# Keeping the scan inputs in SBUF, one array of token columns, positions added by TensorE, and the third part of the modulation moved to a later group

## The chip, the cores and the metric

The kernel runs on one core of a Trainium2 chip. The metric is the device time of one execution in microseconds (us), the median of several runs. In the profile PE is TensorE's matmuls, PEld its weight loads, DVE VectorE, ACT ScalarE, POOL GpSimd, and SP the engine from whose queue nearly every DMA of this kernel is issued.

## The reference: one layer of a hybrid model

2048 latent tokens and 128 context tokens, 1024 wide, pass through one layer. A position embedding is added to the latent tokens only: its first 512 columns depend on the token's grid row (64 tokens share one), the last 512 on its grid column.

```python
x_lat = x_sample + grid_pos_embed(x_sample.shape[1])
sh1, sc1, gt1, sh2, sc2, gt2 = split(silu(c) @ w_ada + b_ada, 6)     # for c and for c_ctx
h = rmsnorm(x, norm_mix) * (1 + sc1) + sh1
u, z_s5, qkv, z_gdn, beta_raw, a_raw = split(h @ w_in)
x = x + gt1 * (concat[s5(u, z_s5), deltanet(conv(qkv), z_gdn, ...)] @ w_out)
h = rmsnorm(x, norm_mlp) * (1 + sc2) + sh2
x = x + gt2 * (square(relu(h @ w_mlp_in)) @ w_mlp_out);  y = rmsnorm(x, norm_final)
```

`s5` is a complex diagonal state-space scan in both directions, `deltanet` a chunked gated delta rule, also in both directions. Everything is fp32; most products are made as three products of a high and a low part (`wh`, `wl` of a weight, `H`, `L` of the tokens).

## The kernel before

Tokens are cut into 17 tiles of 128; tile 16 is the context. The program runs in these stages; the order of instructions inside an engine is set by a scheduler that simulates the program as it is written, so code that moves also moves what is around it.

- **First phase** (`norm_rows`, `first_cols`, `first_pass`). `load_x` brings a tile of rows, adds the row part of the position on POOL (L205, from 64 equal copies of each row that a DMA with a zero step makes, L193) and the column part on DVE (L206). The rows are normalized (L182, L184, L80, L243), transposed on PE (L165), scaled and shifted on DVE (L172), split in high and low parts (L174 on ACT, L175 on POOL or DVE) and written to DRAM in four overlapping arrays per part, one for each later group, whose edge columns are written twice (L259, L263, L266). Eight blocks of tokens, `UBLOCKS` (the first has three tiles, the others two), are then multiplied on PE with the columns for `u` (L289), and ACT copies each result out of PSUM into a buffer `eu` (L292), of which there are two, that a DMA writes to the array `u` in DRAM (L294). The columns for the gates follow (L298 to L313, `gates`). Between the blocks the tables of the S5 scan are built (`s5_setup`, `s5_tables`: L1017 to L1249).
- **Modulation** (`modulation(k, b)`): `silu(c)` for both conditions times a third of `w_ada`, 2048 columns, loaded as 16 pieces of 512 KB (L131), each feeding two matmuls at different column positions of the array (L134). Third 0 runs before the first block, thirds 1 and 2 (`mods`) beside group 0.
- **Group 0** (`group_h`, `group_proj`): the token columns of five tiles are loaded from DRAM (L376), twelve blocks of 128 weight columns are split (L402 to L404) and saved (L387), multiplied (L471) and passed through the convolution (L491 to L503). Beside it run the first S5 scans (L1263 to L1364).
- **Groups 3, 1 and 2**: the same with weights loaded from what was saved, and beside it the inverses of the delta rule in three side sequences `first`, `second`, `third`, of which `third` (`gdn_second`, L775 to L813) uses the one PSUM bank `g3`.
- Then the remaining columns, the delta rule's steps, and the output projection and MLP of all tokens, which take more than half of the time.

All DMAs stand in one queue, SP's, in order: an instruction that waits there holds back all behind it.

Of the kernel before, what the change touches and what calls it, by code (L numbers as in the profile page):

```python
# [67 lines left out]
def setup_first(k):  # L68

    nc = k.nc  # L70
    cst = k.pa.tile([128, 528], F32, name="cst0")
    nc.sync.dma_start(cst, k.I['cst'][:, 512:1040])
    k.pos_c = cst[:, 0:512]
    k.eye16 = cst[:, 512:528]
# [35 lines left out]
def modulation(k, b):  # L110

    nc, I = k.nc, k.I
    bias = k.pm.tile([128, 512], F32, name="mbias")
    nc.vector.memset(bias, 0.0)
    ba = I['b_ada']
    for j in range(4):
        nc.sync.dma_start(bias[32 * j:32 * j + 2], dap(ba, (4 * b + j) * 512, [[0, 2], [1, 512]]))
    nrm = None
    if b != 1:
        nrm = k.pm.tile([128, 512], F32, name="mnorm")  # L120
        nc.vector.memset(nrm, 0.0)
        src = I['norm_mix'] if b == 0 else I['norm_mlp']
        for j in range(2):
            r0 = (64 if b == 0 else 0) + 32 * j
            nc.sync.dma_start(nrm[r0:r0 + 2], dap(src, j * 512, [[0, 2], [1, 512]]))
    ps = k.psM.tile([128, 512], F32, name="gA")
    for kk in range(8):
        for jp in range(2):
            w = k.pmw.tile([128, 2, 512], F32, name="wada")
            c0 = b * 2048 + jp * 1024  # L130
            nc.sync.dma_start(w.rearrange("p j c->p (j c)"), I['w_ada'][0][kk * 128:kk * 128 + 128, c0:c0 + 1024])  # L131
            for i in range(2):
                j = 2 * jp + i
                nc.tensor.matmul(ps[32 * j:32 * j + 32, :], k.csil[:, kk, :], w[:, i, :],  # L134
                                 start=(kk == 0), stop=(kk == 7), tile_position=(0, 32 * j))
            yield None
    rows = bias
# [5 lines left out]
    ps = k.psM.tile([128, 512], F32, name="gA")  # L143
# [52 lines left out]
def load_x(k, t):  # L196
# [13 lines left out]
UBLOCKS = ((16, 0, 1), (2, 3), (4, 5), (6, 7), (8, 9), (10, 11), (12, 13), (14, 15))  # L210


def place(t):

    if t == 16:
        return 0, 1
    return (0, 130 + 128 * t) if t < 4 else (t // 4, 1 + 128 * (t % 4))
# [29 lines left out]
def first_cols(k, tiles, early):  # L247

    nc, S = k.nc, k.S
    H = k.ph.tile([128, 8, 384], FR, name="uH")  # L250
    L = k.ph.tile([128, 8, 384], FR, name="uL")
# [3 lines left out]
    for part, X in (("hH", H), ("hL", L)):  # L255
        X = X.bitcast(F32)
# [13 lines left out]
def first_pass(k, early):  # L270

    nc, S = k.nc, k.S
    pend = []
    cols = first_cols(k, UBLOCKS[0], early)
    for bi, tiles in enumerate(UBLOCKS):
        n = 128 * len(tiles)
        H, L = cols
        if bi < 7:
            cols = first_cols(k, UBLOCKS[bi + 1], early)
        if bi < 6:  # L280
            early.update((t, norm_rows(k, t)) for t in UBLOCKS[bi + 2][:k.ahead])
        yield None
        for ct in range(4):
# [1588 lines left out]
```

## Time and profile before

| | us |
|---|---|
| median of 3 runs | 3313.88 |
| lowest, highest | 3308.87, 3318.6 |
| profiled execution | 3305.27 |
| its span from first to last instruction | 3303.5 |
| PE busy | 2998.2 |
| DVE busy | 2060.2 |

The profiled execution is one run of its own; sums over the trace are made against it and not against the median. "Busy" counts the time in which at least one instruction of an engine is in flight. A row of a group of instructions names line, engine, operation, what is written from what, shape and count, then the busy time and the mean of one, and the idle time of the engine just before them with what ended it.

### The profile page before, as it was taken

The numbers are of one execution on the slowest core, as the hardware profiler recorded it, in microseconds if no ns is written. First come the engines' busy times: TensorE is split into PE (matmuls) and PEld (weight loads), VectorE is DVE, ScalarE is ACT, GpSimd is POOL, SyncE is SP. The second block draws the span as 40 slices with busy tenths as digits, with TensorE's granted clock in tenths as the row PEclk, the third lists the DMA queues.
The fourth block names the chain that finished last, engine by engine and source line by source line (L and its number), as shares of the span: only waits on it lengthen the run. The fifth ranks groups of instructions, "written<-read, shape, count | busy, mean of one in ns | idle before, by whom it ended". The sixth has DMA issues, their size and how long they took to land.

```text
span 3303.5 us, 53799 instructions
## 1 busy us (share of the span) xinstructions
PE 2998.2 (91%) x19962; PEld 2637.7 (80%) x19962; DVE 2060.2 (62%) x4093; ACT 1115.0 (34%) x2517; POOL 1370.5 (41%) x1027
## 2 busy tenths in 40 slices
PE   5775879999798899988999999999999999999998
PEld 3673668787787777977997899898798898899997
DVE  4965587896876775346555368543368652685555
ACT  3432224443443221245323243322243332432332
POOL 3552232433345242155443453434444444554442
PEclk8887889998997999998999999999999999999999
DMA  9899966867677988999333545222435334453322
GB/s 258 197 179 250 335 205 228 266 217 236 201 217 233 285 286 273 345 307 312 107 103 112 156 147 178 81 76 92 143 99 184 112 102 127 155 166 93 99 90 71
DMA packets 573527, 604.69 MB, mean 183 GB/s; under 512 B 163020, under 2 KB 422208, under 8 KB 573264
## 3 DMA queue, kind: packets, MB, share of 16 engines
q1 hardware_dynamic: 573264, 601.25, 59.4%
q8 instruction: 157, 2.57, 0.3%
q14 instruction: 106, 0.87, 0.1%
HBM read 458.99 MB, written 142.14 MB: 182 GB/s over the span
## 4 chain that ended last, share of the span: by engine, by line
PE 56%; DVE 19%; DMA 14%; issue 4%; ACT 3%; POOL 3%; SPq 2%; POOLq 0%; DVEq 0%; ACTq 0%
PE gA L1523 20%; PE gA L1545 18%; PE d L471 6%; PE gA L1437 3%; PE gs L1356 1%; DVE W L738 1%; DVE Tt L1301 1%; DMA x<-in_posr 1%; DVE UB L736 1%; DMA woraw<-in_w_out 1%; DVE S L1338 1%; PE gs L1283 1%; POOL wol L1400 1%; DVE S L1303 1%; DMA s_stab<-WI 1%
## 5 line engine op out<-in xcount | busy, mean ns | idle before, releaser
L1400 POOL TENSOR_TENSOR wol<-woraw,woh 128x512 fp32r<-128x512 f32 x320 | 426.3, 1343 | 679.9 <-ACT woh L1399 669.5
L1530 DVE TENSOR_TENSOR r<-r 128x256 f32<-128x256 f32 (+1 forms) x256 | 290.7, 1168 | 363.8 <-ACT ffH L1529 363.6
L1399 ACT ACTIVATE woh<-woraw 128x512 fp32r<-128x512 f32 x320 | 194.4, 628 | 794.6 <-PE gA L1545 462.0
L1545 PE MATMUL gA<-woh,ffH 128*128 128x512 f32 x1088 | 426.8, 392 | 8.8 <-ACT r L1527 4.8
L1545 PE MATMUL gA<-woh,ffL 128*128 128x512 f32 x1088 | 425.3, 391 | 1.1 <-DVE ffL L1531 1.1
L1545 PE MATMUL gA<-wol,ffH 128*128 128x512 f32 x1088 | 424.2, 390 | 0.0
L1550 DVE TENSOR_TENSOR acc<-acc,gA 128x512 f32<-128x512 f32 x510 | 336.1, 681 | 123.7 <-PE gA L1545 123.6
L1400 POOL TENSOR_TENSOR wil<-wiraw,wih 128x1024 fp32r<-128x1024 f32 x128 | 318.9, 2491 | 148.5 <-PE gA L1523 111.6
L1523 PE MATMUL gA<-htH,wih 128*128 128x256 f32 (+1 forms) x2048 | 286.9, 292 | 6.0 <-DVE acc L1550 4.0
L1523 PE MATMUL gA<-htL,wih 128*128 128x256 f32 (+1 forms) x2048 | 284.8, 290 | 0.0
L1523 PEld LDWEIGHTS gA<-htH,wih 128*128 128x128 f32 x2048 | 273.0, 192 | 13.1 <-DVE acc L1550 6.3
L1523 PE MATMUL gA<-htH,wil 128*128 128x256 f32 (+1 forms) x2048 | 282.0, 290 | 0.0
L1523 PEld LDWEIGHTS gA<-htL,wih 128*128 128x128 f32 x2048 | 270.5, 192 | 0.9
L1523 PEld LDWEIGHTS gA<-htH,wil 128*128 128x128 f32 x2048 | 268.6, 191 | 0.1
L471 PE MATMUL d<-hH,wh 128*128 128x258 f32 (+3 forms) x1152 | 213.4, 327 | 51.5 <-DMA wh<-s_wc 15.9
L1545 PEld LDWEIGHTS gA<-woh,ffH 128*128 128x128 f32 x1088 | 204.8, 188 | 52.7 <-ACT r L1527 6.1
L471 PEld LDWEIGHTS d<-hH,wh 128*128 128x128 f32 x1152 | 180.2, 206 | 74.0 <-issue 31.4
L1545 PEld LDWEIGHTS gA<-wol,ffH 128*128 128x128 f32 x1088 | 204.7, 188 | 43.2
L1545 PEld LDWEIGHTS gA<-woh,ffL 128*128 128x128 f32 x1088 | 204.9, 188 | 41.4 <-DVE ffL L1531 1.9
L471 PE MATMUL d<-hL,wh 128*128 128x258 f32 (+3 forms) x1152 | 213.1, 320 | 2.7 <-DMA hL<-s_hL 2.7
L471 PE MATMUL d<-hH,wl 128*128 128x258 f32 (+3 forms) x1152 | 209.4, 319 | 4.6 <-DMA wl<-s_wc 4.6
L471 PEld LDWEIGHTS d<-hH,wl 128*128 128x128 f32 x1152 | 178.0, 201 | 18.2 <-issue 10.3
(387 smaller groups left out, 5340.0 us busy)
## 6 DMA issues: line engine op xcount, KB each, us to landing
wiraw<-in_w_mlp_in SPq DMA_DIRECT2D x128, 512.0 KB
woraw<-in_w_mlp_out SPq DMA_DIRECT2D x256, 256.0 KB
wl<-s_wc SPq DMA_DIRECT2D x68, 512.0 KB
wh<-s_wc SPq DMA_DIRECT2D x68, 512.0 KB
wada<-in_w_ada SPq DMA_DIRECT2D x48, 512.0 KB
KVr<-s_kv SPq DMA_DIRECT2D x34, 512.0 KB
Qr<-s_qkv SPq DMA_DIRECT2D x32, 512.0 KB
woraw<-in_w_out SPq DMA_DIRECT2D x64, 256.0 KB
```

The source lines that it names most:

```text
L471: nc.tensor.matmul(ps[:, 0:w], W_[:, kk, :], X_[kk][:, f:f + w], start=(n == 0), stop=(n == 23))
L736: nc.vector.tensor_tensor(tv, W[:, 0:i + 1, i:i + 1].to_broadcast([128, i + 1, m]), U2[:, i, None, i + 1:32].to_broadcast([128, i + 1, m]) ...
L738: nc.vector.tensor_tensor(wv, wv, tv, op=OP.subtract)
L1283: nc.tensor.matmul(ps[64 * par:64 * par + 64, 0:272], WI[:, d, ri, g, 64 * par:64 * par + 64], ub[:, 2 * g + par, :], start=True, stop=Tru ...
L1301: V.tensor_tensor(Tt.rearrange("p j (a s)->p j a s", a=8), sview(S, kk, [[0, 2], [272, 8], [16, 17]]), TB8[:, :, :, None].to_broadcast([12 ...
L1399: nc.scalar.activation(h[:, i:i + n], w, AF.Copy)
L1400: sub.tensor_tensor(l[:, i:i + n], w, h[:, i:i + n].bitcast(F32), op=OP.subtract)
L1437: nc.tensor.matmul(ps, X[:, q, s], W[:, kk, :], start=(q == 0 and m == 0), stop=(q == 7 and m == 2))
L1523: nc.tensor.matmul(ps[b][:, 0:w], W[:, kk, :], X[:, kk, b * w:b * w + w], start=(m == 0), stop=(m == 23))
L1530: nc.vector.tensor_tensor(r[:, 0:w], r[:, 0:w], r[:, 0:w], op=OP.mult)
L1545: nc.tensor.matmul(ps, X[:, s], W[:, hf], start=(m == 0), stop=(m == 3 * FB - 1))
L1550: nc.vector.tensor_tensor(accs[i][:, c], accs[i][:, c], ps, op=OP.add)
```

## The change

Five edits.

- `U`, one tile of [128, 4, 8, 272], takes all results for `u`; it is written to DRAM in two halves, after blocks 4 and 8, as rows of 128 and 144 values in place of rows of 32 (or 16).
- The high and low token columns stand in one array each (`hH`, `hL`, 2177 columns); edges are no longer written twice.
- `load_x` no longer loads copies of position rows. Two matmuls with a broadcast column of the identity as weights spread two position rows over 64 tokens each, a third with the identity passes on the column part, and DVE adds both halves from PSUM.
- The first block is split: tile 16 alone, then eight pairs, nine blocks.
- Third 2 of the modulation leaves group 0 and runs beside group 3, in 32 pieces of 256 KB with three buffers and one matmul each, in the PSUM bank `g3`; `third` waits until it is done. The pool `pw` of split weights is made after the first phase and not before it.

```diff
@@ load_x
     nc.sync.dma_start(x, I['x_sample'][0, t * 128:(t + 1) * 128])
-    pr = k.px.tile([128, 512], F32, name="posr", bufs=2)
-    load_posr(k, pr, t)
-    nc.gpsimd.tensor_tensor(x[:, 0:512], x[:, 0:512], pr, op=OP.add)
-    nc.vector.tensor_tensor(x[:, 512:1024], x[:, 512:1024], k.pos_c, op=OP.add)
+    for hf in range(2):
+        ps = k.psA.tile([128, 512], F32, name="gA")
+        if hf:
+            nc.tensor.matmul(ps, k.ident, k.pos_c, start=True, stop=True)
+        else:
+            for j in range(2):
+                nc.tensor.matmul(ps[64 * j:64 * j + 64], k.ident[0:32, 2 * t + j:2 * t + j + 1].to_broadcast([32, 64]), k.pos_r,
+                                 start=True, stop=True, tile_position=(0, 64 * j))
+        nc.vector.tensor_tensor(x[:, 512 * hf:512 * hf + 512], x[:, 512 * hf:512 * hf + 512], ps, op=OP.add)
-UBLOCKS = ((16, 0, 1), (2, 3), (4, 5), (6, 7), (8, 9), (10, 11), (12, 13), (14, 15))
+UBLOCKS = ((16,), (0, 1), (2, 3), (4, 5), (6, 7), (8, 9), (10, 11), (12, 13), (14, 15))
@@ first_cols
         for (i, t, m) in runs(tiles):
-            g, c0 = place(t)
-            nc.sync.dma_start(S[f'{part}{g}'][:, :, c0:c0 + 128 * m], X[:, :, 128 * i:128 * (i + m)])
-            if t + m in (4, 8, 12):
-                e = 128 * (i + m)
-                nc.sync.dma_start(S[f'{part}{g + 1}'][:, :, 0:1], X[:, :, e - 1:e])
-            if t in (4, 8, 12):
-                c0 = 642 if t == 4 else 513
-                nc.sync.dma_start(S[f'{part}{g - 1}'][:, :, c0:c0 + 1], X[:, :, 128 * i:128 * i + 1])
+            c0 = place(t)
+            nc.sync.dma_start(S[part][:, :, c0:c0 + 128 * m], X.bitcast(F32)[:, :, 128 * i:128 * (i + m)])
@@ first_pass
+    U = k.pu.tile([128, 4, 8, 272], F32, name="eu")
...
-            u = k.pe.tile([128, 8, 48], F32, name="eu")
-            nc.scalar.activation(u[:, :, 0:n // 8], ps[:, 0:n].rearrange("p (c l)->p l c", l=8)[:, ::-1], AF.Copy)
-            for (i, t, m) in runs(tiles):
-                nc.sync.dma_start(S['u'][ct * 128:(ct + 1) * 128, :, 16 * t:16 * (t + m)], u[:, :, 16 * i:16 * (i + m)])
+            c0 = 16 * tiles[0]
+            nc.scalar.activation(U[:, ct, :, c0:c0 + n // 8], ps[:, 0:n].rearrange("p (c l)->p l c", l=8)[:, ::-1], AF.Copy)
+            if bi in (4, 8):
+                cs = slice(0, 128) if bi == 4 else slice(128, 272)
+                nc.sync.dma_start(S['u'][ct * 128:(ct + 1) * 128, :, cs], U[:, ct, :, cs])
...
-        if bi % 2:
+        if bi % 2 or bi == 8:
             gates(k, ab, pend)
@@ modulation
+    n = 2 if b < 2 else 1
     for kk in range(8):
-        for jp in range(2):
-            w = k.pmw.tile([128, 2, 512], F32, name="wada")
+        for jp in range(0, 4, n):
+            w = k.pmw.tile([128, n, 512], F32, name="wada")
...
@@ program
-            k.pw = pool(st0, "pw", 2)
...
+            k.pw = pool(st0, "pw", 2)
...
-                third, second, first = Side(3), Side(4), Side(2)
+                mods = []
+                third, second, first = Side(3, (), lambda: not mods), Side(4), Side(2)
...
-                    mods = seq(modulation(k, 1), modulation(k, 2))
+                    mod1 = modulation(k, 1)
                     for _ in seq(group_h(k, 0, True), group_proj(k, 0, range(8, 20))):
-                        advance(mods, 3)
+                        advance(mod1, 2)
...
+                k.pmw = k.pm = pool(sm, "pmw2", 3)
+                k.psM, k.mp, k.mb = k.psI, "g3", ("wada", "wada")
+                mods.append(modulation(k, 2))
                 for gi in (3, 1, 2):
                     for _ in seq(group_h(k, gi, True), group_proj(k, gi, range(8, 20))):
                         for s in (first, second, third, scans):
                             s.go()
+                        if mods:
+                            advance(mods[0], 3)
+                    if mods:
+                        drain(mods.pop())
+                        sm.close()
```

Where the instructions stand. The first place is SP's queue at the end of the first phase: the last writes of `u`, and what stands ahead of the loads of group 0's columns (`hH`). Before (nine more lines follow before the first load of `hH`):

```order
L294 DMA s_u<-eu 1024x1x32 x4
L131 DMA wada<-in_w_ada 128x1024 x2
L117 DMA mbias<-in_b_ada 2x512 x2
L1217 DMA s_stab<-WI 128x1024
L117 DMA mbias<-in_b_ada 2x512 x2
L131 DMA wada<-in_w_ada 128x1024
L1249 DMA s_stab<-KK 128x1x128 x7
L1225 DMA s_stab<-WI 128x2x512
L1249 DMA s_stab<-KK 128x1x128
L131 DMA wada<-in_w_ada 128x1024 x2
L336 DMA s_gb<-gb 128x64
L1040 DMA SPl<-s_sp 128x1408
```

And in the change:

```order
L270 DMA s_hL<-uL 1024x1x256
L298 DMA s_u<-eu 1024x1x144 x2
L340 DMA s_gb<-gb 128x64
L298 DMA s_u<-eu 1024x1x144 x2
L375 DMA hH_3114<-s_hH 128x128
L375 DMA hH_3114<-s_hH 128x513
L375 DMA hH_3115<-s_hH 128x128
L375 DMA hH_3115<-s_hH 128x513
L375 DMA hH_3116<-s_hH 128x128
```

The loads of `hH` now stand right behind the writes of `u`; pieces of `w_ada`, the table writes (`s_stab`) and the S5 loads (`SPl`, `ub`, `WI`, `CA`) stood ahead of them before. Four blocks of weights for group 0 are also loaded and split, and two of them saved, inside the first phase.

The second place is PE at the same point: the last transposes of the gates (`abT`), and the first matmuls of group 0 (`hH` with `wh`). Before:

```order
L308 MATMUL d<-ident,abT 128x32 x2
L1238 MATMUL gs<-CA,bbar 32x128 x32
L134 MATMUL gA<-wada,csil 32x512 x10
L1283 MATMUL gs<-ub,WI 64x272 x10
L134 MATMUL gA<-wada,csil 32x512 x2
L1283 MATMUL gs<-ub,WI 64x272 x6
L134 MATMUL gA<-wada,csil 32x512 x2
L1351 MATMUL gs<-ub,WT 128x272 x2
L134 MATMUL gA<-wada,csil 32x512 x4
L471 MATMUL d<-hH_2982,wh 128x388
```

And in the change:

```order
L302 MATMUL d<-uH,ab_290 32x256 x8
L304 MATMUL d<-uL,ab_291 32x256 x8
L312 MATMUL d<-ident,abT 128x32 x2
L470 MATMUL d<-hH_3114,wh 128x388
L470 MATMUL d<-hH_3114,wh 128x258
L470 MATMUL d<-hH_3114,wh 128x388
```

Before, a part of the tables, 18 matmuls of the modulation and the first of a scan stood between the two; now nothing does.

The third place is PE early in group 3. The names `hH` and `wl` are the columns and the low part of a weight. Before:

```order
L471 MATMUL d<-hH_4742,wl 128x258
L471 MATMUL d<-hH_4743,wl 128x258
L471 MATMUL d<-hH_4744,wl 128x258
L471 MATMUL d<-hH_4745,wl 128x258
L471 MATMUL d<-hH_4746,wl 128x258
L471 MATMUL d<-hH_4747,wl 128x258
```

And in the change, where `g` is the bank `g3`:

```order
L140 MATMUL g_4929<-wada,csil 32x512
L470 MATMUL d<-hH_4788,wl 128x258
L470 MATMUL d<-hH_4789,wl 128x258
L470 MATMUL d<-hH_4790,wl 128x258
L470 MATMUL d<-hH_4791,wl 128x258
L140 MATMUL g_4929<-wada,csil 32x512
L470 MATMUL d<-hH_4792,wl 128x258
```

The 32 matmuls of third 2 of the modulation now stand at 25 places between those of group 3; the first matmul of the side sequence `third` (L774 in the change) comes after the last of them.

## Rows read from the trace of the kernel before

**Rows 1.** Windows by stage: PE, PEld, DVE, ACT, POOL busy (count); PEclk, DMA, GB/s

```profile
0.00:100.00 100.00, 50.18 (x216) 31.16 (x217) 57.39 (x184) 32.91 (x49) 33.42 (x29) 0.82 0.92 248
100.00:180.00 80.00, 66.13 (x527) 60.24 (x525) 77.46 (x160) 35.97 (x68) 56.60 (x40) 0.93 0.82 197
180.00:280.00 100.00, 75.36 (x644) 71.17 (x644) 65.02 (x144) 33.38 (x73) 51.62 (x53) 0.86 0.92 167
280.00:327.00 47.00, 22.50 (x138) 7.03 (x138) 19.39 (x61) 12.52 (x25) 6.47 (x46) 0.67 0.98 317
327.00:505.00 178.00, 148.62 (x798) 114.47 (x799) 125.11 (x293) 43.68 (x82) 47.62 (x29) 0.90 0.82 269
505.00:627.00 122.00, 112.07 (x829) 100.17 (x829) 108.34 (x300) 57.79 (x178) 45.11 (x39) 0.94 0.68 222
```

**Rows 2.** DMA of the first phase, 0 to 283 us, share of 16 engines

```profile
DMA packets 100520, 57.69 MB, mean 204 GB/s; under 512 B 65176, under 2 KB 91340, under 8 KB 100499
...
q1 hardware_dynamic: 100499, 57.43, 88.8%
```

**Rows 3.** Waits, 0 to 284 us: us in total, times, longest

```profile
ACT eu L292 <- DMA s_u<-eu: 53.4, 10, 10.8
...
POOL x L205 <- DMA x<-in_x_sample: 19.4, 4, 10.0
```

**Rows 4.** Instructions on tile x, first phase: duration ns, first, last start

```profile
L182 ACT ACTIVATE hrow<-x x17: 1042/1057/1107, 8.1 to 199.4; 128x1024 f32<-128x1024 f32 x17
```

**Rows 5.** DMA, 279 to 282 us, when almost only writes of u run

```profile
DMA packets 2088, 0.30 MB, mean 100 GB/s; under 512 B 2079, under 2 KB 2079, under 8 KB 2088
...
q1 hardware_dynamic: 2088, 0.30, 64.0%
```

**Rows 6.** Costliest groups of the first phase, DVE and POOL

```profile
L205 POOL TENSOR_TENSOR x<-x,posr 128x512 f32<-128x512 f32 x16 | 24.9, 1554 | 25.7 <-DMA x<-in_x_sample 19.4 <-PE gA L165 2.8 <-DMA wada<-in_w_ada 1.4
...
L206 DVE TENSOR_TENSOR x<-x,cst 128x512 f32<-128x512 f32 x16 | 14.8, 926 | 9.1 <-DMA x<-in_x_sample 8.6 <-DMA posr<-in_posr 0.5
```

**Rows 7.** Page, section 5: a DVE addition out of PSUM

```profile
L1550 DVE TENSOR_TENSOR acc<-acc,gA 128x512 f32<-128x512 f32 x510 | 336.1, 681 | 123.7 <-PE gA L1545 123.6
```

**Rows 8.** Timeline of PE inside a block: start, length, what, count

```profile
222.06 1.11 PE L289 MATMUL d<-uL,wh 128*128 128x256 f32 x8
223.01 1.11 PE L289 MATMUL d<-uH,wl 128*128 128x256 f32 x8
...
229.53 1.47 PE L165 MATMUL gA<-ident,hrow 128*128 128x128 f32 x12
```

**Rows 9.** Timeline of PE: single slots of the modulation in group 0

```profile
382.15 1.05 PE L134 MATMUL gA<-wada,csil 128*32 128x512 f32 x4
383.13 1.22 PE L471 MATMUL d<-hH,wh 128*128 128x258 f32 x8
...
466.41 1.07 PE L134 MATMUL gA<-wada,csil 128*32 128x512 f32 x8
```

**Rows 10.** Timeline of PE from the first phase to group 0

```profile
280.25 0.31 PE L308 MATMUL d<-ident,abT 32*128 32x32 f32 x2 [0.30 <-ACT abT L302]
...
298.07 3.22 PE L134 MATMUL gA<-wada,csil 128*32 128x512 f32 x8 [6.14 <-DMA wada<-in_w_ada]
...
327.17 6.44 PE L471 MATMUL d<-hH,wh 128*128 128x388 f32 x21 [8.90 <-DMA hH<-s_hH]
```

**Rows 11.** Timeline of SP from the first phase to group 0

```profile
280.58 1.12 SPq L131 DMA_DIRECT2D wada<-in_w_ada  x2
...
284.89 6.39 SPq L1249 DMA_DIRECT2D s_stab<-KK  x7
...
311.66 7.35 SPq L376 DMA_DIRECT2D hH<-s_hH  x8
```

**Rows 12.** Waits, 284 to 500 us

```profile
PEld gA L134 <- DMA wada<-in_w_ada: 20.2, 9, 7.9
```

**Rows 13.** Instructions of L775, the first of the side sequence third

```profile
L775 PE MATMUL g<-RW,UC x544: 191/191/258, 622.6 to 1240.9; 32*32 32x32 f32 x182
```

More of the change, by code (lines that the diff above doesn't have):

```diff
@@ L73, in setup_first @@
     k.pos_c = cst[:, 0:512]
+    k.pos_r = k.pa.tile([32, 512], F32, name="posr")
+    nc.sync.dma_start(k.pos_r, k.I['posr'])
     k.eye16 = cst[:, 512:528]
@@ L112, in modulation, with vectors @@
     nc, I = k.nc, k.I
[L113 to L126, printed above, removed]
-    for kk in range(8):
-        for jp in range(2):
-            w = k.pmw.tile([128, 2, 512], F32, name="wada")
[L130 to L133, printed above, removed]
+    def vectors():
+        bias = k.pm.tile([128, 512], F32, name=k.mb[0])
+        nc.vector.memset(bias, 0.0)
+        for j in range(4):
+            nc.sync.dma_start(bias[32 * j:32 * j + 2], dap(I['b_ada'], (4 * b + j) * 512, [[0, 2], [1, 512]]))
+        nrm = None
+        if b != 1:
+            nrm = k.pm.tile([128, 512], F32, name=k.mb[1])
+            nc.vector.memset(nrm, 0.0)
+            src = I['norm_mix'] if b == 0 else I['norm_mlp']
+            for j in range(2):
+                r0 = (64 if b == 0 else 0) + 32 * j
+                nc.sync.dma_start(nrm[r0:r0 + 2], dap(src, j * 512, [[0, 2], [1, 512]]))
+        return bias, nrm
+    if b < 2:
+        bias, nrm = vectors()
+    ps = k.psM.tile([128, 512], F32, name=k.mp)
+    n = 2 if b < 2 else 1
+    for kk in range(8):
+        for jp in range(0, 4, n):
+            w = k.pmw.tile([128, n, 512], F32, name="wada")
+            c0 = b * 2048 + jp * 512
+            nc.sync.dma_start(w.rearrange("p j c->p (j c)"), I['w_ada'][0][kk * 128:kk * 128 + 128, c0:c0 + 512 * n])
+            for i in range(n):
+                j = jp + i
                 nc.tensor.matmul(ps[32 * j:32 * j + 32, :], k.csil[:, kk, :], w[:, i, :],
@@ L249, in first_cols @@
     nc, S = k.nc, k.S
-    H = k.ph.tile([128, 8, 384], FR, name="uH")
-    L = k.ph.tile([128, 8, 384], FR, name="uL")
+    H = k.ph.tile([128, 8, 256], FR, name="uH")
+    L = k.ph.tile([128, 8, 256], FR, name="uL")
     for i, t in enumerate(tiles):
@@ L355, in group_h @@
             segs.append((w, 128 * m, 128 * t))
-            for u in range(t, t + m):
-                g, c = place(u)
-                if u > t and parts[-1][1] == g:
-                    parts[-1][3] += 128
-                else:
-                    parts.append([w, g, c, 128])
-                w += 128
+            parts.append((w, place(t), 128 * m))
+            w += 128 * m
         blocks = [(0, w, w, segs)]
@@ L374, in group_h @@
                 nc.gpsimd.memset(x[:, z:z + 1], 0.0)
-            for (a, g, c, m) in parts:
-                nc.sync.dma_start(x[:, a:a + m], S[f'{part}{g}'][:, q, c:c + m])
+            for (a, c, m) in parts:
+                nc.sync.dma_start(x[:, a:a + m], S[part][:, q, c:c + m])
         yield None
@@ L399, in split_w @@
     wh = p.tile([128, 8, 128], FR, name="wh" + nm)
-    wl = p.tile([128, 8, 128], FR, name="wl" + nm, bufs=k.wlb if p is k.pw else 1)
+    wl = p.tile([128, 8, 128], FR, name="wl" + nm, bufs=1 if nm else k.wlb)
     w = k.pwr.tile([128, 8, 128], F32, name="wraw")
@@ L514 @@
     'tz': [512, T], 'wc': [24, 2, 128, 1024],
[L515 removed]
+    'hH': [128, 8, 2177], 'hL': [128, 8, 2177],
     'qkv': [17, 128, 1536], 'zg': [512, T],
```

31 lines of the change are left out of this document (15 added, 16 removed).

## Prediction

> **What bounds the kernel now.** I read the windows by stage first [rows 1]. Of the 3303.5 us the change touches the first 627. In the first 280 us the DMA engines are busy 92, 82 and 92% of the time, PE 50, 83 and 75%, DVE 57, 97 and 65%. So DMA is full at the beginning and at the end, and DVE alone in the middle, where the S5 tables are set up. Then come 47 us in which PE does little (22.5 us, at a clock of 0.67) and DMA is at 98%, then group 0 until 505 us with no engine full (PE 83%, DMA 82%), then group 3 with PE at 92% and DVE at 89%.
>
> The waits say what the DMA holds up: ACT stood 53.4 us, in 10 waits, at the copy of `u` out of PSUM, until a write of `u` had freed one of two buffers [rows 3]. The front is not what is late there: the last tile is normalized at 199.4 us [rows 4], 80 us before the last block is done. The last transposes of the phase stand at 280.25 us, the first matmul of group 0 at 327.17 [rows 10], and the loads that it waits for were issued only at 311.66, behind pieces of `w_ada` and table writes [rows 11]. These two places, the writes of `u` and the 47 us, carry the forecast.
>
> **First phase: what leaves the DMA engines.** Their time in 283 us is 0.888 x 283 = 251 us [rows 2].
>
> - Writes of `u`: 36 DMAs of 1024 pieces make 36,864 packets, 32,768 of 128 B and 4096 of 64 B. In a stretch with little else, 2088 packets took 64% of 3 us on 16 engines [rows 5], so 0.64 x 3 x 16 / 2088 = 14.7 ns each and 34 us in all. The mean packet of the phase, 40 ns [rows 2], is the other end: 92 us. I take 34. In their place come 8 DMAs of 1024 packets of 512 or 576 B, 4.5 MB. No row shows these alone; at the phase's mean of 204 GB/s [rows 2] they cost 22 us, at the 317 of the next stage [rows 1] 14. I take 18. Net -16.
> - Position rows: 32 DMAs of 128 KB, 4.2 MB: 13 to 21 us by the same two rates. I take 16; the one load of 64 KB that stays is nothing.
> - Edge columns: 12 DMAs of 1024 packets of 4 B at 14.7 ns: 11 us (at the mean packet 31).
> - Added: four weight blocks, 2.1 MB, are read and two saved, 2.1 MB, inside the phase: 13 to 21 us, I take 16. It is taken from group 0.
>
> So 251 - 43 + 16 = 224 us, and at the same share 224 / 0.888 = 252 us in place of 283.
>
> The Trainium skill, page "DMA: Bandwidth & Descriptors", section Specifications, puts line rate at transfers of 512 B and more, and 27 GiB/s on an engine. By that, as an estimate, the new writes of `u` would take 10 us and not 18, and the phase would gain 9 more. The row of 128 B packets (14.7 ns, 8.7 GB/s on an engine) agrees on the small side, and no row here shows the other.
>
> **What is late next.** PE. A block of two tiles has 112 matmuls at 8 in 0.95 us, 13.3 us, and 16 transposes at 0.122, 2.0 us [rows 8]. The positions add, per tile, a pair of matmuls at two column positions and one full matmul of 512 columns in fp32. The nearest row is a pair of the modulation (four records, since an fp32 matmul leaves two), which holds PE for 383.13 - 382.15 = 0.98 us, and two pairs at four positions 1.07 us [rows 9]. With 0.98 for the pair and for the full one: 1.96 us a tile, 31 us for 16. It is not below 8 (16 slots of which half hide under neighbours) nor above 39 (two slots as long as the 1.22 us of the row that follows). The split first block adds 112 matmuls of 128 columns and shortens 112 others: between 0 and 13.3 us, I take 4, since the narrower ones together stream as many columns as before. PE was busy 191.7 us in 280 [rows 1]; now 227. In 252 us that is 90%, as in group 3, so it fits and hardly more. DVE adds 32 times 681 ns out of PSUM [rows 7], 21.8 us, loses 14.8 [rows 6], and does one more set of gates, some 6 us: 213 of 252, 85%. POOL loses 24.9 us [rows 6], part of which it spent waiting for x (19.4 us, rows 3). I take 250 for the phase: -30, from 0 to -50.
>
> **Between the phase and group 0.** 46.9 us lie between the last transposes and the first matmul of group 0 [rows 10]. In the change nothing stands between them on PE, and on SP the loads of `hH` follow the last write of `u`. Before, 15.5 us passed from the first such load to the first matmul [rows 10, 11]; PE can start on the first piece, so 5 to 15, I take 8. What PE did in the 47 us comes back in group 0: 22.5 x 0.67 = 15 us at full clock. Third 2 of the modulation leaves it: 16 pairs at 0.98, 15.7 us of PE, and 8.4 MB, 26 to 31 us of DMA at 317 and 269 GB/s. The two cancel on PE, DMA is lighter, and group 0 keeps its 178 us: 8 + 178 = 186, rounded up to 187 for the scan, whose loads now stand behind `hH`. That replaces 225: -38. Were DMA all that held group 0, it would come near PE's 148 us at group 3's share of 92%, 161: -56. If the returned work finds no room: -24.
>
> **Group 3.** It gets 32 matmuls at 25 places between its own. A place costs 0.98 us whether two or three stand there [rows 9]: 24.5 us; if they gathered in fours, 8 x 1.07 = 9; if each stood alone, 31. PE was idle 10 us of 122 [rows 1], and about half of that takes some up: +20. Three buffers give each piece three places' time, 122 / 32 x 3 = 11 us, to arrive, more than the longest wait for a piece before (7.9 us) [rows 12]. Behind a waiting matmul stands all of PE, and behind the load of a piece that waits for its buffer the next weights in SP's queue. `third` now starts after group 3; it started at 622.6 before [rows 13], when group 3 was nearly done, so this costs nothing.
>
> **Sum.** -30 - 38 + 20 = -48. The profiled execution took 3305.27 us, 8.6 less than the median of 3313.88; so 3257, and 3266 for the median. What follows is moved earlier and stays as it is.
>
> **Rivals.**
>
> 1. DMA was all that held both stages: phase -50, group 0 -56, group 3 +10: -96, 3218. For it: 98% in the 47 us and the 53.4 us of ACT. Against it: PE at 90% of the phase.
> 2. PE becomes the bound of the phase: each of the 16 pairs and 16 full matmuls costs its neighbours more than 0.98, up to two slots of 1.22 us a tile, and waits for the three PSUM banks that they share with the transposes come on top, so that the phase gains 5; group 0 -30, group 3 +25: -10, 3304. The Trainium skill, page "TensorEngine Tiling (Array Packing)", section Key Properties, says that changing the tiling mode drains TensorE; the pairs and the 25 places each do so twice. Against it: the 0.98 us were measured between full matmuls, so it holds such a change already.
> 3. Slower: PE waits for its pieces in group 3. If each of 25 places also waits the mean of before, 20.2 / 9 = 2.2 us [rows 12], the group costs 25 x 3.2 = 80: -30 - 38 + 80 = +12, 3326. It decides from a group 3 that is 78 us longer. Against it are the 11 us a piece has.
> 4. It does not do what it says: the writes of `u` were not what held the blocks, PE waits for the gates' copies instead, and the phase keeps its length; group 0 -25, group 3 +20: -5, 3309.
>
> **How the numbers follow.** Chances: forecast 0.50 (its own range 3240 to 3292), rival 1 0.15, rival 2 0.18, rival 3 0.07, rival 4 0.10. What a measurement of this kernel can tell from no change is about 0.3%, 10 us, so faster means below 3304. The forecast and rival 1 are faster, rival 2 a little more than half, rival 4 a third: 0.79. Same: 0.15. Slower: most of rival 3, 0.06. The range goes from 3218 (the end of rival 1) to 3312, which leaves out rival 3 and a little of rivals 1 and 4.
>
> **What would show it.** No wait of ACT for a write of `u`; the last transposes of the gates near 250 us with PE at about 90% in the last 70; the first matmul of group 0 within 15 us of them; the end of group 0 near 437 us and of group 3 near 579; PE's waits for `wada` in group 3 under 10 us. A first phase over 270 us, or over 150 us of group 3, would make the forecast wrong.

## The result and the profile after

The changed kernel takes 3344.12 us (median of 4 runs, 3337.43 to 3348.62), the kernel before in the same session 3311.38. The ratio is 1.0102, 95% interval 1.0072 to 1.0133: slower by 1%, where 3266 was forecast. The profiled execution has a span of 3346.2 us.

These are the windows of the changed kernel by stage (columns as in [rows 1]): three of the first phase, then groups 0, 3 and 1, each to its last projection matmul, and four stretches that end at projection matmul 2304 (the end of group 2), 2700, 3000 and 3456, the last.

```profile
0.00:100.00 100.00, 80.07 (x380) 49.70 (x381) 59.80 (x193) 28.56 (x49) 29.47 (x22) 0.81 0.73 213
100.00:180.00 80.00, 67.57 (x559) 56.48 (x557) 70.83 (x151) 35.73 (x69) 48.79 (x35) 0.91 0.51 155
180.00:280.00 100.00, 82.23 (x606) 64.65 (x606) 58.72 (x150) 47.24 (x84) 44.80 (x35) 0.85 0.70 211
302.20:464.10 161.90, 132.81 (x749) 106.85 (x750) 110.54 (x254) 41.70 (x81) 37.11 (x30) 0.87 0.81 276
464.10:608.30 144.20, 144.20 (x920) 106.20 (x918) 119.32 (x355) 64.58 (x190) 43.86 (x37) 1.00 0.78 250
608.30:801.60 193.30, 164.00 (x1416) 138.60 (x1415) 153.91 (x392) 75.88 (x212) 77.92 (x67) 0.84 0.70 216
801.60:971.20 169.60, 146.30 (x1296) 127.53 (x1296) 137.45 (x352) 68.52 (x194) 56.44 (x50) 0.88 0.63 194
971.20:1117.60 146.40, 129.44 (x1070) 108.96 (x1069) 94.24 (x247) 52.98 (x142) 66.57 (x55) 0.80 0.64 202
1117.60:1310.00 192.40, 155.92 (x1243) 132.96 (x1241) 129.44 (x319) 44.23 (x108) 58.14 (x56) 0.88 0.84 277
1310.00:1457.00 147.00, 137.79 (x888) 130.63 (x888) 43.80 (x107) 33.18 (x101) 25.31 (x26) 0.99 0.92 322
```

The five stretches of the kernel before that answer to the last five:

```profile
629.00:762.40 133.40, 121.80 (x897) 105.44 (x896) 111.28 (x309) 59.52 (x175) 38.91 (x35) 0.93 0.73 235
762.40:920.00 157.60, 137.62 (x1322) 122.14 (x1321) 121.13 (x314) 65.81 (x186) 63.34 (x59) 0.91 0.73 228
920.00:1036.50 116.50, 100.39 (x951) 87.83 (x950) 93.82 (x234) 50.42 (x134) 52.96 (x39) 0.93 0.70 221
1036.50:1239.30 202.80, 181.04 (x1516) 149.23 (x1515) 136.56 (x336) 57.36 (x147) 74.06 (x71) 0.90 0.88 277
1239.30:1413.80 174.50, 160.50 (x1190) 148.38 (x1189) 76.55 (x187) 40.29 (x119) 41.33 (x37) 0.98 0.87 300
```

- **First phase.** It ends at 296.2 us and not at 280.6 [rows 10]: +16, with DMA at 73, 51 and 70% in place of 92, 82 and 92 [rows 1].
- **To the end of group 0:** at 464.1 instead of 498.0, so 167.9 us from the end of the phase in place of 217.4. Here lies the gain: -50.
- **Group 3:** 144.2 us, with PE full at full clock, against 131.0: +13. The kernel is now 21 us ahead.
- **Group 1 and on:** group 1 takes 193.3 us against 133.4, the five stretches 848.7 against 784.8: +64. What follows takes the same time in both, so the end is 43 us late.

PE does about the same work in the five stretches. Busy time times granted clock, summed over the rows, is 652 us at full clock before and 644 after; what is lost to waits and to the lower clock is 133 us before and 205 after. Of these 72 us more, 32 are time without a matmul (115 us in place of 83); the rest, some 40, is the lower clock, an estimate, since the clock of a row is its mean.

The wait of ACT for a write of `u` [rows 3] is gone. In its place stand waits along one chain through all engines (changed kernel, 100 to 282 us; total, times, longest). `hrow` is a tile of rows, `uH` and `uL` its high and low part, and `gA` one of the three PSUM banks that the transposes (L173) and the positions (L215) share:

```profile
POOL uL L183 <- ACT uH L182: 55.5, 10, 8.2
...
ACT uH L182 <- DVE hrow L180: 27.8, 16, 8.4
DVE hrow L180 <- PE gA L173: 23.9, 5, 6.3
...
PE gA L215 <- DVE hrow L180: 13.8, 4, 4.8
```

The last tile is normalized at 274.1 us, 22 us before the phase ends, where it was 199.4, 80 us before [rows 4]; this row gives the durations, then the first and last start:

```profile
L190 ACT ACTIVATE hrow<-x x17: 1042/1057/1062, 7.9 to 274.1; 128x1024 f32<-128x1024 f32 x17
```

From the last transposes to the first matmul of group 0 PE now waits 6.0 us [rows 10]:

```profile
295.93 0.31 PE L312 MATMUL d<-ident,abT 32*128 32x32 f32 x2 [0.46 <-ACT abT L306]
302.23 4.12 PE L470 MATMUL d<-hH,wh 128*128 128x388 f32 x13 [6.00 <-DMA hH<-s_hH]
```

In group 3 the moved third costs PE its slots and hardly a wait (the 64 records of its 32 matmuls, then the idle time before them):

```profile
L140 PE MATMUL g<-wada,csil x64: 592/605/617, 469.3 to 584.5; 128*32 128x512 f32 x64
...
  DMA wada<-in_w_ada: 0.9, 1
```

### The profile page after: what moved, and what is told of

The parts are those of the page before. It is cut to its first block, busy times and chain, and to the rows that moved or that the text cites. A ratio compares the mean times of both kernels' runs of the same rounds, so it can differ in the third digit from the quotient of the medians.

```text
span 3346.2 us, 54116 instructions
## 1 busy us (share of the span) xinstructions
PE 3073.3 (92%) x20170; PEld 2672.7 (80%) x20170; DVE 2058.3 (62%) x4136; ACT 1122.2 (34%) x2525; POOL 1350.7 (40%) x1011
## 4 chain that ended last, share of the span: by engine, by line
PE 61%; DVE 16%; DMA 12%; issue 4%; POOL 3%; ACT 3%; SPq 1%; POOLq 0%; DVEq 0%; ACTq 0%
PE gA L1522 18%; PE gA L1544 18%; PE d L470 9%; PE gA L1436 3%; PE d L292 2%; PE gs L1355 1%; DMA wada<-in_w_ada 1%; DMA s_rw<-UB 1%; DVE S L1337 1%; DVE Tt L1300 1%; DMA x<-in_posr 1%; POOL wol L1399 1%; DMA wh<-s_wc 1%; PE gs L1282 1%; DVE otmp L1456 1%
## 5 line engine op out<-in xcount | busy, mean ns | idle before, releaser
L470 PEld LDWEIGHTS d<-hL,wh 128*128 128x128 f32 x1152 | 176.0, 199 | 32.7 <-DMA hL<-s_hL 18.4
```

What stands on the lines that cost most here:

```text
L470: nc.tensor.matmul(ps[:, 0:w], W_[:, kk, :], X_[kk][:, f:f + w], start=(n == 0), stop=(n == 23))
```

## The experiments

All were timed beside the kernel before, in groups; "ratio" is to its runs, with the 95% interval. The end of the phase is that of the last transposes of the gates in the profiled run (before: 280.6; changed: 296.2). Kernels of different groups were timed at different times, and the median of the kernel before lay between 3306 and 3312 us; a difference of some microseconds between two of them says nothing.

**First group: undo one part of the change, or do its wait alone.**

`no_move`: in `program`, third 2 as before.

```diff
-    mod1 = modulation(k, 1)            # and third 2 beside group 3
+    mods = seq(modulation(k, 1), modulation(k, 2))
     ...
-    third = Side(3, (), lambda: not mods)
+    third = Side(3)
```

> The changed kernel with third 2 of the modulation back beside group 0 and without the wait of `third`; everything else of the change stays. Theory 1 (the late loss comes from the moved third: PE's order of the delta rule's work in group 1 changes with it): groups 3 and 1 together take about 270 us instead of 337, group 0 gets 15 to 25 us longer, the whole is 25 to 50 us below the changed kernel, about 3300. Theory 2 (the late loss comes from the first phase's edits, which only shift everything in time): groups 3 and 1 stay near 325, the whole is within 10 us of the changed kernel, about 3340.

3326.7 us, 1.0049 (1.0032 to 1.0067), 17 below the changed kernel, where 25 to 50 were expected. Phase 296.4 as there; groups 3 and 1 take 275 us in place of 337, and group 0 takes 187 again. So much of the late loss hangs on the moved third, not on the first phase. Not all of it: the five stretches take 812 us, where the changed kernel takes 849 and the kernel before 785.

`no_pe_pos`: in `load_x`, positions as before.

```diff
-    for hf in range(2): ...                       # matmuls, adds out of PSUM
+    pr = k.px.tile([128, 512], F32, name="posr", bufs=2)
+    load_posr(k, pr, t)
+    nc.gpsimd.tensor_tensor(x[:, 0:512], x[:, 0:512], pr, op=OP.add)
+    nc.vector.tensor_tensor(x[:, 512:1024], x[:, 512:1024], k.pos_c, op=OP.add)
```

> The changed kernel with positions added as before (copies of rows by DMA, POOL and DVE adds, no matmuls). Theory 1 (positions on PE share three PSUM banks with the transposes and lengthen the first phase): the phase ends near 265 us instead of 294, the whole is 20 to 30 us below the changed kernel, about 3318, the late loss stays. Theory 2 (the phase is long for another reason, the split first block or the loss of running ahead): the phase stays within 10 us of 294, the whole within 10 of 3344.

3328.0 us, 1.0056 (1.0037 to 1.0075). The phase ends at 271.7, 24.5 earlier, as theory 1 has it; whether by the banks is not told by this run. Little of it is passed on: 17.6 us now lie between the phase and group 0, which ends 9 us earlier (454.9). The late loss stays (groups 3 and 1: 321 us).

`no_move_no_pos`: both undone.

> The changed kernel with both undone: what stays is u kept on chip, single arrays of token columns, the split first block. If the two losses are separate and add, the whole is 45 to 80 us below the changed kernel, 3264 to 3299, below the kernel before. If u and the arrays are what lengthens the first phase, it is not below 3311.

3302.5 us, 0.9984 (0.9968 to 1.0000). The two losses add: 17 and 16 us apart, 42 together, a little under the 45 to 80 expected. But 7 us (273.8) is all that the rest of the change gives the phase.

`hold_only`: the kernel before, with the wait and nothing else.

```diff
-    third = Side(3)
+    held = [1]; third = Side(3, (), lambda: not held)   # cleared after group 3
```

> The kernel before with one line more: `third` may not start before group 3 is done. No work is added or moved between stages otherwise. If the wait of `third` alone makes the loss of the changed kernel in group 1, group 1 takes 150 us or more instead of 133 and the whole is 20 to 50 us above before, 3330 to 3360. If the wait is harmless (in the kernel before `third` starts at 622.6 us, 6 us before group 3 ends), the whole is within 10 us of before, 3301 to 3321.

3345.6 us, 1.0121 (1.0093 to 1.0149). A wait that takes no engine's time, of work that began 6 us before group 3 ended [rows 13], costs 39 us.

**Second group: what in the first phase, and is any order as bad?**

`half_pos`: `no_move`, with the column half of the position added on POOL from SBUF.

```diff
-    nc.tensor.matmul(ps, k.ident, k.pos_c, start=True, stop=True)    # and its add on DVE
+    nc.gpsimd.tensor_tensor(x[:, 512:1024], x[:, 512:1024], k.pos_c, op=OP.add)
```

> As no_move (third 2 back beside group 0), but only the row half of the position goes through TensorE; the column half is added on POOL from SBUF, without a matmul and without a PSUM bank. Theory 1 (each position array on PE costs the phase by its slot and its share of the three banks): about half of the 22 to 25 us that the positions cost comes back, the phase ends near 284 us and the whole near 3315. Theory 2 (the pair with the changed tile position is what costs, or POOL becomes the late engine): the phase stays above 290.

3312.3 us, 1.0015 (1.0000 to 1.0029); the phase ends at 290.7, on the border of the two theories, and doesn't decide.

`small_u`: `no_move_no_pos`, with `u` written from the chip after each block.

```diff
-    if bi in (4, 8): cs = slice(0, 128) if bi == 4 else slice(128, 272)
+    cs = slice(c0, c0 + n // 8)
```

> As no_move_no_pos, but u is written from its buffer on chip after every block, in 36 DMAs of 64 or 128 B pieces as in the kernel before, and no copy waits for such a write. If DMA traffic still bounds the phase without the wait (my prediction), the phase ends near 290 us instead of 274. If it does not (VectorE is at 39 of 40 us from 100 to 180), the phase stays within 5 us of 274 and the whole within 15 of 3302.

3301.5 us, 0.9973 (0.9958 to 0.9988), phase 278.4. First `small_u`, then `no_move_no_pos`: DMA of the first phase and the share of the 16 engines.

```profile
DMA packets 90957, 60.42 MB, mean 217 GB/s; under 512 B 52017, under 2 KB 81195, under 8 KB 90935
q1 hardware_dynamic: 90935, 60.15, 80.8%
```

```profile
DMA packets 56608, 57.13 MB, mean 209 GB/s; under 512 B 15624, under 2 KB 46847, under 8 KB 56587
q1 hardware_dynamic: 56587, 56.86, 71.2%
```

In `small_u` the engines are busy 0.808 x 278 - 0.712 x 274 = 30 us longer each, and the phase is 5 us longer. (Not all of the 30 is the price of small pieces: the window of `small_u` holds 3.3 MB more, mostly since `no_move_no_pos` writes the second half of `u` only behind its phase.) DMA does not bound the phase.

`first_rate3`: the kernel before, with one number changed.

```diff
-    third, second, first = Side(3), Side(4), Side(2)
+    third, second, first = Side(3), Side(4), Side(3)
```

> The kernel before with one number changed: the side sequence `first` takes three steps where it took two. No work is added or removed; only the order of the side work between groups 3 and 2 moves a little. If the order alone is worth tens of microseconds (hold_only: +39), this lies off 3306 by 10 us or more, up or down. If hold_only was special, because of its wait, this stays within 10 us of 3306.

3308.2 us, 0.9994 (0.9981 to 1.0008): no difference. So not every shift costs, and the wait was special; how, the third group shows.

`scan_rate3`: `no_move_no_pos`, likewise.

```diff
-    scans = Side(2, [s5_part(k, hb) for hb in range(8)])
+    scans = Side(3, [s5_part(k, hb) for hb in range(8)])
```

> As no_move_no_pos with one number changed: the scans take three steps where they took two. No work is added or removed. If order is worth tens of microseconds, it lies off 3302 by 10 us or more; earlier scans fill group 0 and group 3, where PE had 43 and 5 us without work, so rather below, about 3285; if order matters only through the wait of `third`, within 10 us of 3302.

3325.5 us, 1.0037 (1.0016 to 1.0058), 23 above its base, on the side opposite to what I expected. The loss lies in group 0, which takes 213.6 us in place of 195.0; from its end to the last projection matmul both take the same time, 934 and 935 us.

**Third group: the wait alone, at two lengths, and the front.** Count the 3456 projection matmuls in PE's order in 36 blocks of 96, numbered from 0, and look where the matmuls of `third` (the inverses) and of the scans stand; each is counted to the block of the projection matmul before it. In the kernel before, 256 of the 1904 inverse matmuls stand in block 31. In `hold_only` and the changed kernel none stands behind block 30. I call these orders late and early. The line was drawn from the runs made so far.

`hold_8` and `hold_11`: the kernel before, `third` held for 8 or 11 of the 14 steps of group 3. Inverses in blocks 31 and 32: 336 and 0.

```diff
+    held[0] += 1                                  # each step of a group
     ...
-    third = Side(3)
+    third = Side(3, (), lambda: held[0] >= 8)     # 11 in hold_11
```

> The kernel before, with `third` held for the first 8 of the 14 steps of group 3. Its first batch then stands one block later on PE, but all that follows (the second batch in blocks 18 and 19 of 96 projection matmuls, the scans) stands where it stood. If the loss of hold_only comes from the shifted order after group 3, this stays within 10 us of before, about 3306. If the delay of the first batch itself costs, it is 20 to 40 above.

> The same held for 11 steps. From here on the second batch begins one block earlier on PE (80 matmuls in block 17), and the scans of the blocks behind it shift too, as in hold_only. If that order is the loss, 3335 to 3355, 30 to 45 above hold_8. If it is not, within 10 us of hold_8.

3291.7 us, 0.9947 (0.9929 to 0.9964), and 3350.2, 1.0122 (1.0099 to 1.0144). One number in one lambda is worth 58 us. `hold_8` is faster than the kernel before, by more than the 10 us within which it was expected. This gain is not one of the late stretches: the 15 us between the two profiled runs lie behind the last projection matmul (1875 us to the end in place of 1890), and no run shows why. The same five stretches, first `hold_8`, then `hold_11`:

```profile
619.50:748.70 129.20, 121.29 (x935) 106.21 (x935) 104.74 (x302) 59.43 (x173) 41.47 (x36) 0.97 0.75 247
748.70:921.30 172.60, 148.57 (x1330) 130.23 (x1330) 120.33 (x326) 67.11 (x188) 64.82 (x62) 0.84 0.70 212
921.30:1037.40 116.10, 101.91 (x952) 89.05 (x951) 92.33 (x233) 50.94 (x134) 50.43 (x38) 0.91 0.71 222
1037.40:1232.40 195.00, 170.03 (x1384) 137.50 (x1382) 138.93 (x325) 52.96 (x135) 67.59 (x64) 0.89 0.83 269
1232.40:1413.20 180.80, 171.23 (x1317) 159.61 (x1317) 81.66 (x199) 43.46 (x130) 48.53 (x46) 0.98 0.92 312
```

```profile
623.90:776.60 152.70, 138.47 (x1130) 119.16 (x1130) 114.18 (x325) 65.98 (x187) 50.70 (x47) 0.92 0.70 229
776.60:943.50 166.90, 147.20 (x1320) 127.61 (x1320) 123.39 (x321) 69.20 (x193) 57.74 (x55) 0.88 0.70 214
943.50:1107.70 164.20, 131.48 (x1115) 109.83 (x1114) 119.06 (x273) 61.48 (x167) 73.17 (x60) 0.80 0.61 187
1107.70:1325.40 217.70, 184.82 (x1579) 159.57 (x1577) 153.78 (x375) 48.83 (x122) 71.01 (x66) 0.87 0.84 277
1325.40:1469.20 143.80, 128.01 (x777) 118.20 (x776) 36.97 (x92) 29.99 (x91) 19.44 (x20) 0.99 0.87 290
```

PE's work at full clock is 654 and 650 us; lost are 139 and 196. The early order ends with a shorter last stretch (143.8 against 180.8), since it has done the inverses already, and pays more than that in the stretches where it did them. One such place in `hold_11`: PE waits 6.6 us for a load of the inverses,

```profile
1065.74 0.64 PE L775 MATMUL g<-RW,UC 32*32 32x32 f32 x8 [6.61 <-DMA RW<-s_rw]
```

and then works for 20 us without a gap at half the clock (windows of 10 us):

```profile
1050.00:1060.00 10.00, 9.13 (x48) 6.59 (x46) 3.27 (x8) 6.58 (x17) 1.11 (x2) 1.00 0.40 123
1060.00:1070.00 10.00, 4.26 (x52) 3.05 (x53) 0.44 (x1) 0.57 (x2) 4.07 (x6) 0.62 0.77 192
1070.00:1080.00 10.00, 10.00 (x75) 6.97 (x75) 1.85 (x3) 3.69 (x13) 8.39 (x7) 0.50 0.73 234
1080.00:1090.00 10.00, 10.00 (x66) 6.13 (x63) 2.20 (x8) 3.12 (x10) 2.31 (x2) 0.51 0.74 241
1090.00:1100.00 10.00, 10.00 (x130) 8.68 (x130) 7.62 (x17) 2.98 (x8) 1.06 (x2) 1.00 0.66 146
```

The granted clock is 1.00, falls in the window with the wait, and is 0.50 and 0.51 (1.2 of 2.4 GHz) in the two behind it. The Trainium skill, page "TensorE: Matmul & The Clock Gate", section "HAM oscillation — how this bites in real kernels", says that a wait for data lets the clock fall and the next work starts cold; the rows agree.

`ahead_pe_pos`: `no_move`, positions on PE, with the rows of the block after next ahead.

```diff
         if bi < 8:
             cols = first_cols(k, UBLOCKS[bi + 1], early)
+        if bi < 7:
+            early.update((t, norm_rows(k, t)) for t in UBLOCKS[bi + 2])
```

> As no_move, positions on PE as in the changed kernel, but the rows of the block after next are loaded, added and normalized in the program ahead of a block's matmuls, so that the position matmuls stand one block earlier on PE. Theory 1 (the positions cost the phase because each tile passes through PE's order twice and the front can't run ahead): the phase ends near 278 us instead of 296. Theory 2 (PE's slots, DVE's adds out of PSUM and the three banks cost it): the phase stays above 290.

3299.1 us, 0.9959 (0.9933 to 0.9985): 28 below `no_move`. The phase ends at 270.4, with every position matmul still on PE, 26 us earlier than in `no_move`; at the end of group 0 (483.7 and 490.2) 6.5 of them are left, so the phase explains the 28 only in part. The last tile is normalized 42 us before that:

```profile
L187 ACT ACTIVATE hrow<-x x17: 1040/1056/1063, 7.8 to 228.3; 128x1024 f32<-128x1024 f32 x17
```

The matmul of the column part, in the changed kernel and here (shortest, median, longest ns of the 32 records of 16 matmuls; under each the longest of the waits of PE and its weight loads for another engine before it):

```profile
L215 PE MATMUL gA<-cst,ident x32: 590/1061/1224, 8.4 to 272.7; 128*128 128x512 f32 x32
...
  DVE hrow L180: 29.5, 9
```

```profile
L212 PE MATMUL gA<-cst,ident x32: 590/592/1222, 8.5 to 223.5; 128*128 128x512 f32 x32
...
  DVE kf L1082: 0.8, 1
```

It doesn't only wait less: its median falls from 1061 to 592 ns. In both traces a record takes 1061 to 1224 ns at a granted clock of 0.50 and 590 to 700 at 1.00. From 100 to 180 us DVE, the third engine of the row, is now full:

```profile
100.00:180.00 80.00, 67.28 (x541) 56.35 (x540) 79.35 (x170) 37.27 (x72) 49.36 (x37) 0.89 0.54 171
180.00:280.00 100.00, 80.79 (x716) 71.11 (x714) 72.54 (x193) 40.30 (x83) 36.37 (x41) 0.97 0.68 193
```

`ahead_copies`: `no_move_no_pos` with the same step ahead.

> As no_move_no_pos, with the same step ahead. The front ran ahead by itself there (last tile normalized 57 us before the end of the phase), so the phase should stay within 5 us of 274. After group 3 its delta rule stands on PE nearly as in the kernel before; if that order is the better one, the whole comes to about 3285, below both kernels; if not, 3300.

3306.5 us, 0.9987 (0.9972 to 1.0003), phase 274.5. Where the front ran ahead already, the step changes nothing. DVE has less to do here than in `ahead_pe_pos`, and the phase is 4 us longer, so a full DVE from 100 to 180 us is not yet what sets the end of the phase; what does is not shown. Of the late orders it is not one of the better.

**Fourth group: the changed kernel itself, with the order of either kind.**

`move_rate4` and `move_rate5`: the changed kernel; `third` is let go when third 2 is done, fed at 4 or 5 pieces a step.

```diff
-    advance(mods[0], 3)
+    advance(mods[0], 5)                 # 4 in move_rate4
+    if mods[0].gi_frame is None: held.clear()
```

> The changed kernel, third 2 beside group 3 in bank g3, but four pieces a step in place of three, and `third` let go as soon as they are done (about step 9 of 14) and not at the end of the group. PE's order is then still of the early kind: inverses and scans packed into groups 1 and 2, all done before projection block 31. Theory 1 (the loss is the order, as between hold_8 and hold_11): within 12 us of the changed kernel, 3332 to 3350. Theory 2 (the length of the hold or the 32 matmuls): 10 to 20 below it.

> The same with five pieces a step, so that `third` is let go at step 7. One number differs from move_rate4. PE's order is now of the late kind, as before: inverses in blocks 31 and 32, scans in 30 to 32. Theory 1: 30 to 45 below move_rate4, 3298 to 3312, with the moved third and its matmuls still in group 3. Theory 2 (the moved matmuls or bank g3 cost the time later): within 10 us of move_rate4.

3339.8 us, 1.0090 (1.0069 to 1.0111), and 3309.7, 1.0005 (0.9987 to 1.0024). Inverses behind block 30: 0 and 288. Both have the moved third in bank `g3` beside group 3; one number and with it the order differs, and 30 us. The profiled run of `move_rate5` (3328.5) is its slowest of ten, so the traces of this pair show only 10 us of them, between group 0 and the last projection matmul.

`ahead_hold_8`: `ahead_pe_pos` with the hold of 8 steps that was harmless in the kernel before. Here it gives the early order.

```diff
-    third = Side(3)
+    third = Side(3, (), lambda: held[0] >= 8)
```

> As ahead_pe_pos (3299), with `third` held for 8 steps of group 3. In the kernel before that hold was harmless; here it makes the early kind of order (all inverses and scans done before block 31). If the order decides and not the hold, 3325 to 3350. If a hold of 8 steps is harmless by itself, 3290 to 3310.

3333.0 us, 1.0076 (1.0053 to 1.0100), 34 above `ahead_pe_pos`: the order, and not the hold.

**Last: all of the change with the two faults mended, and what closed the gap.**

`all_late`: the changed kernel with the step of `ahead_pe_pos`, five pieces a step, and third 1 at one piece a step beside group 0, which gives the late order.

```diff
+    early.update((t, norm_rows(k, t)) for t in UBLOCKS[bi + 2])
     ...
-    advance(mod1, 2)
+    advance(mod1, 1)
     ...
-    advance(mods[0], 3)
+    advance(mods[0], 5)
+    if mods[0].gi_frame is None: held.clear()
```

> All five edits of the change, with the two faults mended: rows of the block after next are normalized ahead (as in ahead_pe_pos), third 2 is fed at five pieces a step and lets `third` go when it is done; second and first thirds beside group 0 at one piece a step, which gives PE an order of the late kind. Theory 1: phase 270 us, group 3 about 15 us longer for its 32 matmuls, the late loss gone: 3280 to 3300, below both kernels. If positions and moved third have other costs later, 3310 or more.

3292.7 us, 0.9957 (0.9939 to 0.9975). Phase 270.1, group 3 152.0. Every edit of the change is in it, and it is faster than the kernel before.

`arrays_hold_8`: `hold_8` with the single arrays of token columns.

```diff
-    **{f'{p}{g}': [128, 8, w] for p in ('hH', 'hL') for g, w in enumerate((643, 514, 514, 513))},
+    'hH': [128, 8, 2177], 'hL': [128, 8, 2177],
```

> The kernel before with only the single arrays of token columns (no edge columns, other loads), and the hold of 8 steps of hold_8. Late order. If the edge columns or the four arrays cost something in the first phase or before group 0, the gap of 45 us shrinks and the whole is 3270 to 3285. If not, 3285 to 3300 as hold_8.

3285.2 us, 0.9931 (0.9906 to 0.9957): the lowest of all, though its interval overlaps that of `hold_8`. The gap before group 0 stays, 43.3 us.

`pool_moved`: the kernel before, with the pool of split weights made after the phase. A single run, without an interval.

```diff
     setup_common(k, st0)
-    k.pw = pool(st0, "pw", 2)
     ...
+    k.pw = pool(st0, "pw", 2)
     ss, sp2, sp1 = ExitStack(), ExitStack(), ExitStack()
```

> The kernel before with one edit: the pool of split weights is made after the first phase. If that alone moves the loads of group 0 forward in SP's queue, the gap between the phase and group 0 falls from 47 us to under 25. If u on chip (no writes and no freed buffer in between) does it, the gap stays above 40.

The gap is 45.6 us (one run: 3310.6). So neither the arrays nor the pool alone closed it. What is left is `u` on chip, with the split first block, which frees the memory for it; neither was tried apart, nor the edits in pairs. And it is closed only in part: with a phase of 270 to 274 us (`no_pe_pos`, `no_move_no_pos`, `ahead_pe_pos`, `all_late`) 17 to 18 us are left of 46.6.

## Why the prediction was wrong

**First phase, -30 forecast, +16 measured.** Two steps failed. The first is "at the same share 224 / 0.888 = 252 us", which took DMA for the bound. The engines' time did fall, and further than I had it, from 251 to 0.660 x 296 = 195 us:

```profile
DMA packets 61231, 58.39 MB, mean 197 GB/s; under 512 B 15278, under 2 KB 53100, under 8 KB 61208
q1 hardware_dynamic: 61208, 58.10, 66.0%
```

But the phase did not follow: `small_u` puts 30 us of DMA time back and loses 5, and without the position matmuls the phase is 7 us shorter and not 30. In the middle DVE was full, 77.46 of 80 us [rows 1], and is so again where the front runs ahead (79.35 in `ahead_pe_pos`; 70.83 in the changed kernel, which waits). I had averaged it away as "213 of 252, 85%". One term was mis-sized besides: by their packets in the trace the old writes of `u` took 43 us (19.5 ns for one of 128 B) and not 34. The 18 us for the new ones were near: in `no_move_no_pos` a packet of 576 B took 33.8 ns. By the Trainium skill's line rate from 512 B and 27 GiB/s (page "DMA: Bandwidth & Descriptors", section Specifications) it would take 20 ns, as an estimate; the trace does not agree, and either way the phase gains nothing. The 53.4 us that ACT waited [rows 3] were nearly free, as rival 4 had it, though not for its reason: PE's weight loads wait 27.7 us for the gates' copies before and 4.8 in the changed kernel. The second failed step is the 31 us of PE slots for the positions. Slots are not what they cost: `ahead_pe_pos` has the same matmuls and a phase of 270.4. In the changed kernel each tile passes through PE's order twice, for the position and for the transposes, behind the matmuls of the block before, so that the front no longer ran ahead. Rival 2 had the direction, and of its two causes the rows show one: PE waits 13.8 us before the position matmuls, and its weight loads 15.7, until DVE has emptied a bank of the transposes. But `ahead_pe_pos` has the same slots and the same three banks and not this wait, so what makes the banks scarce is the place in the order.

The Trainium skill, page "TensorEngine Tiling (Array Packing)", section Key Properties, has a change of tiling mode drain TensorE, which I weighed as a price of the pairs. `ahead_pe_pos` has all 16 pairs in a phase of 270.4, where `ahead_copies`, without them, has 274.5: no such price shows here.

**To the end of group 0, -38 forecast, -50 measured.** Right in what happens: the gap is 6.0 us where 8 was forecast, group 0 takes 161.9 where 178 was, and third 2 is what made room (`no_move`: 187.4). That the gap is so short is luck, since it comes with the late end of the phase. With a phase of 272 and 270 us, nearer to the 250 that I took, `no_pe_pos` and `all_late` need 183 and 182 us from there to the end of group 0: -34 and -35.

**Group 3, +20 forecast, +13 measured.** Right, also in that PE's waits for its pieces are under 10 us: 0.9 in all. Rival 3, which gave the right sign, had the wrong mechanism.

**After group 3, 0 forecast, +64 measured.** This is the step that gave the wrong sign: "`third` now starts after group 3; it started at 622.6 before [rows 13], when group 3 was nearly done, so this costs nothing", and "What follows is moved earlier and stays as it is". The start did not become later: 610.2 against 622.6. But the wait changed the order in which a scheduler put 1904 inverse matmuls and the scans among the projection matmuls. Of the 19 kernels compared (the two of the change among them), seven have no inverse behind block 30: ratios 1.0037 to 1.0122. The others have them there: 0.9931 to 1.0015, but for `no_move`, 1.0049. Its first phase is that of the changed kernel, but it ends group 0 8 us ahead of the kernel before, so that does not explain it. The three pairs that differ in little else, `hold_8` and `hold_11`, `move_rate5` and `move_rate4`, `ahead_pe_pos` and `ahead_hold_8`, differ by 58, 30 and 34 us. So the order makes a good part of the 64, but not all: with a late order the five stretches still take 812 us in `no_move`, 819 in `move_rate5` and 805 in `all_late`, against 785 before and 794 in `hold_8`.

**What stays open.** That one and the same work in another order takes 30 to 58 us more is shown by the three pairs; which part of the order does it, and through which wait, is not. The line at block 30 does not sort every run: `scan_rate3` is on the early side and loses nothing after group 0. PE loses the time to many waits of 2 to 12 us and to the low clock behind them, and no experiment took one of these away alone. Nor is it shown why, from the end of group 0 to the last projection matmul, the kernels with `u` on chip and a late order take some 935 us (`no_move_no_pos`, `small_u`, `ahead_pe_pos`) where `hold_8` takes 920 and the kernel before 916: they end group 0 at 478 to 486 us in place of 493 to 498, and lose all of that again here.

## What to carry to other kernels

Where a scheduler places side work among the main work, a wait in one side sequence is a change of the whole order: read where the side work stands before and after. Here that alone was worth about 1 to 2%. A stage that gives an in-order engine a second pass over each tile has to be issued a block ahead, or the front waits for the back. A high busy share does not show a bound; taking it away does: here the share of the DMA engines in the first phase fell from 89% to 66%, and the phase became longer. And of what a stage gains only what the next ones pass on counts: of 26 us in the first phase, 6.5 were left at the end of group 0.

## What was not expected of the hardware

A wait is paid twice. The matmul of the column part, the same instruction on the same operands, has a median of 592 ns where the front runs ahead (granted clock 1.00) and 1061 where PE waits before it (0.50), and a wait of 6.6 us was followed by 20 us of work at a granted clock of 0.50. In the five late stretches of the changed kernel the waits and the lower clock are 205 of 849 us, in the kernel before 133 of 785.
